# Moving the weight buffers by 32 bytes in SBUF, in a two-block fp32 transformer kernel

## The chip, the cores and the metric

The kernel runs on one core of one Trainium2 chip. The metric is the device time of one execution in microseconds (us). Lower is better.

## What is computed

Two blocks of a transformer-like network on 256 tokens of width 1024, all in fp32. Most of the work is products of the activations with large weight matrices: the input projections, the output projections and five gated feed-forward layers (`f0` to `f4`, hidden width 2816). Cut to what matters:

```python
h = h + (g_a * ya + g_b * yb) @ w_o[l]
hn = rmsnorm(h, norm_ffn_g[l])
gu = hn @ w_ffn_in[l]
g, up = jnp.split(gu, 2, axis=-1)
h = h + (jax.nn.silu(g) * up) @ w_ffn_out[l]
```

Between them stand a banded attention, a gated linear recurrence, a spatial gating unit and a stick-breaking attention. They are small beside the weight products.

## The kernel before

**Splitting.** fp32 accuracy is had from three matmuls per product. Each weight tile `w` is split into `h` (its rounding to float32r, ScalarE, L162) and `l = w - h` (VectorE, L163); activations are split the same way into `xh`, `xl` (or into halves of the four `rr` tables). `mm3` (L212) then issues `h*xh`, `h*xl` and `l*xh` into one PSUM bank. Nearly every matmul of the program is one of these three, issued by `mm` (L210).

**Which operand is which.** In `pe_k`, `pe_a` and `pe_r` (L217 to L238) a 128-column slice of `h` or `l` is the stationary operand, and 256 columns of `xh`, `xl` or `rr` are the moving one. In `pe_nat` and `pe_rn` (L240, L789) it is the other way round: activations are stationary and 512 columns of `h` or `l` move. Half of the kv stage (L916 to L921) moves 256 columns of `h` or `l`. The profile's names put the moving operand first: `wk<-xh,h` moves `xh` over weights `h`.

**Order.** A plan (`make_plan`, L67) fixes the order of all weight tiles. `load` (L139) brings them by DMA on the SP queue, 1 MB (two chunks) at a time, into one of three `raw` tables; `prep` (L149) splits one chunk of 1024 columns per partition into one of eight `h` and eight `l` tables, up to seven chunks ahead of TensorE. One chunk feeds 24 matmuls of `mm3`.

**SBUF layout.** `setup` (L318) allocates the tables of the pool `const` one behind the other, each starting at a multiple of 32 bytes in every partition; the pools `raw` and `hl` (L1243, L1244) follow it. Counted as the remainder of 256 of the start address, before the change:

```
par (896 bytes)                                  128
x0..x3, xh, xl, rr0..rr3, sa                       0
sb, sc, sd, sf, sg, sh, ident, ones              128
rt, r1t, rkv, rckv                               160
half (96 bytes)                                  128
ntri, nones, identb, maskb, lamt                 224
raw, h, l (all buffers)                           64
```

All tables of `x`, `xh`, `xl`, `rr`, `raw`, `h` and `l`, and all their slices that a matmul reads (512 or 1024 bytes apart), are multiples of 256 bytes apart, so one remainder holds for every matmul on them. `ntri` and `nones` are the 128x128 weights of the running sums in `stick` (L1129, L1131); they are used against the `rr` tables.

Of the kernel before, what the change touches and what calls it, by code (L numbers as in the profile page):

```python
# [106 lines left out]
class Builder:  # L107
# [210 lines left out]
    def setup(self):  # L318
        nc, dram = self.nc, self.dram
        self.P = self.sb("par", [128, 224])[:, 0:NPAR]  # L320
        self.X = [self.sb(f"x{p}", [128, 2, 256]) for p in range(4)]
        self.XS = (self.sb("xh", [128, 8, 256], F32R), self.sb("xl", [128, 8, 256], F32R))
        self.RR = [self.sb(f"rr{i}", [128, 8, 256], F32R) for i in range(4)]
        self.SA = self.sb("sa", [128, 2080])[:, 0:8 * 259]
        self.SL = {c: self.sb("s" + c, [128, 2048]) for c in "bcdfgh"}
        self.ident = self.sb("ident", [128, 128])
        self.ones = self.sb("ones", [128, 128])
        self.mhalf = self.sb("mhalf", [128, 2])
        self.Rt = self.sb("rt", [128, 256])
        self.R1 = self.sb("r1t", [128, 256])  # L330
        self.Rkv = self.sb("rkv", [128, 256])
        self.rckv = self.sb("rckv", [128, 16])[:, 0:2]
        self.v2 = self.sb("v2", [128, 2])
        self.rc = self.sb("rc", [128, 2])
        self.tiny = self.sb("tiny", [128, 1])
        self.c8 = self.sb("c8", [128, 8])
        self.nc8 = self.sb("nc8", [128, 8])
        self.half = self.sb("half", [128, 24])
        self.sq = self.view("b", 4)
        nc.scalar.dma_start(self.P, dram["par"])  # L340
        x_load = lambda p: nc.sync.dma_start(self.X[p], dram["x"][:, 2 * p:2 * p + 2, :])
        for f in range(2):
            nc.sync.dma_start(self.X[0][:, f, :], dram["x"][:, f, :])  # L343
        self.warm_up()
        for g in range(2):
            t = self.rawp.tile([128, 2048], F32, tag="raw", name="raw")
            for c in range(2):
                if 2 * g + c:
                    x_load(2 * g + c)
                n = 512 if 2 * g + c == 0 else 1024  # L350
                for o in range(c * 1024, (c + 1) * 1024, n):
                    nc.sync.dma_start(t[:, o:o + n], dram["w"][g, :, o:o + n])  # L352
            self.raw[g] = t
        self.loads = 2
        self.load()
        self.gw = self.SL["h"].rearrange("p (a b) -> p a b", b=128)
        make_identity(nc, self.ident)
        nc.gpsimd.memset(self.ones, 1.0)
        nc.gpsimd.memset(self.mhalf, -0.5)
        nc.gpsimd.memset(self.tiny, 2.0 ** -115)  # L360
# [984 lines left out]
```

## Time and profile before

| | |
|---|---|
| median of 3 runs | 1436.05 us (1435.95 to 1436.43) |
| the profiled execution | 1435.7 us |
| its span, first to last instruction | 1434.0 us |
| mean granted TensorE clock | 0.998 |
| TensorE matmul busy | 1423.5 us, 11548 matmuls |
| VectorE busy | 949.8 us |
| ScalarE busy | 734.9 us |

A matmul's recorded duration is longer than the distance from its start to the next one's, since matmuls are pipelined. What a matmul costs in a dense stream is that distance, here called its step: the length of a piece of the chain divided by its count of matmuls. The recorded duration moves with the step.

### The profile page before, as it was taken

Reading aid. Unit: us, or ns where it says so; the run is one execution under the profiler, and the core shown is the slowest. Engines: PE = TensorE matmul, PEld = TensorE weight load, DVE = VectorE, ACT = ScalarE, POOL = GpSimd, SP = SyncE. Lnnn points to the kernel's source line nnn. Section 1 sums busy time; section 2 is a strip of 40 time slices with the busy share of each in tenths; the row PEclk is TensorE's granted clock in tenths of the full one; section 3 lists DMA queues with packets and bytes.
Section 4 is the critical chain, followed back from the end, with each engine's and each line's share of the span. In section 5 each row is a group of like instructions: output and inputs, shape, how many; then the busy total and the mean of one; then the engine's idle time right before and its main releaser. Section 6 shows DMA issues by size and latency. Waiting matters only on the chain.

```text
span 1434.0 us, 26959 instructions
## 1 busy us (share of the span) xinstructions
PE 1423.5 (99%) x11548; PEld 1384.3 (97%) x11548; DVE 949.8 (66%) x1316; ACT 734.9 (51%) x1094; POOL 24.8 (2%) x57
## 2 busy tenths in 40 slices
PE   9999999999999999999999999999999999999998
PEld 8998989999999999998999999999999998999997
DVE  6976688666557775576776665567655576756663
ACT  5776475544445544455445444446444477544442
POOL 0000000000000000000000000000000000000000
PEclk9999999999999999999999999999999999999999
DMA  8555545454554555546444555544555452445451
GB/s 297 190 204 197 180 171 178 178 204 177 189 193 147 205 182 206 199 165 224 172 163 162 197 186 182 199 178 175 192 199 196 180 176 89 163 155 197 177 190 45
DMA packets 37624, 260.31 MB, mean 182 GB/s; under 512 B 4224, under 2 KB 4608, under 8 KB 7040
## 3 DMA queue, kind: packets, MB, share of 16 engines
q1 hardware_dynamic: 36288, 253.77, 49.5%
q0 software_dynamic: 1072, 4.72, 1.0%
q8 instruction: 90, 1.47, 0.4%
q14 instruction: 30, 0.25, 0.0%
q10 hardware_dynamic: 144, 0.10, 0.0%
HBM read 257.53 MB, written 1.05 MB: 180 GB/s over the span
## 4 chain that ended last, share of the span: by engine, by line
PE 98%; DMA 0%; ACT 0%; DVE 0%; SPq 0%; issue 0%; POOLq 0%; POOL 0%
PE wk L210 62%; PE acc L210 36%; DMA raw<-w 0%; PE acc L521 0%; PE wk L521 0%; ACT sf L959 0%; ACT sd L949 0%; DVE l L163 0%; ACT h L162 0%; SPq L352 0%; SPq L343 0%; DVE sf L950 0%; POOLq L1341 0%; POOL rc L280 0%; ACT sh L1134 0%
## 5 line engine op out<-in xcount | busy, mean ns | idle before, releaser
L163 DVE TENSOR_TENSOR l<-raw,h 128x1024 fp32r<-128x1024 f32 (+1 forms) x479 | 571.1, 1220 | 241.4 <-ACT h L162 241.1
L210 PE MATMUL wk<-xh,h 128*128 128x256 f32 x2272 | 641.1, 282 | 1.8 <-ACT h L162 1.8
L210 PE MATMUL wk<-xh,l 128*128 128x256 f32 x2272 | 638.2, 281 | 0.5 <-DVE l L163 0.5
L210 PE MATMUL wk<-xl,h 128*128 128x256 f32 x2272 | 637.8, 281 | 0.0
L162 ACT ACTIVATE h<-raw 128x1024 fp32r<-128x1024 f32 (+1 forms) x479 | 486.1, 1045 | 61.2 <-PE acc L210 28.8
L210 PEld LDWEIGHTS wk<-xl,h 128*128 128x128 f32 x2272 | 433.2, 191 | 0.5
L210 PEld LDWEIGHTS wk<-xh,h 128*128 128x128 f32 x2272 | 427.4, 188 | 4.5 <-issue 2.0
L210 PEld LDWEIGHTS wk<-xh,l 128*128 128x128 f32 x2272 | 429.8, 189 | 0.9 <-DVE l L163 0.9
L210 PE MATMUL acc<-rr,h 128*128 128x256 f32 x2016 | 359.8, 281 | 0.0
L210 PEld LDWEIGHTS acc<-rr,h 128*128 128x128 f32 x2016 | 309.9, 189 | 1.9 <-issue 1.9
L210 PE MATMUL acc<-rr,l 128*128 128x256 f32 x1008 | 282.8, 281 | 0.0
L210 PEld LDWEIGHTS acc<-rr,l 128*128 128x128 f32 x1008 | 189.9, 188 | 0.0
L738 ACT ACTIVATE sa<-sa 128x256 f32<-128x256 f32 x110 | 45.5, 418 | 271.9 <-DVE sa L306 271.8
L309 ACT ACTIVATE rr<-sa 128x256 fp32r<-128x256 f32 (+1 forms) x122 | 52.7, 439 | 185.3 <-DVE sa L743 128.9
L306 DVE TENSOR_TENSOR sa<-wk,rt 128x512 f32<-128x512 f32 x92 | 62.3, 687 | 79.3 <-PE wk L210 62.6
L310 DVE TENSOR_TENSOR rr<-sa,rr 128x256 fp32r<-128x256 f32 (+1 forms) x122 | 54.1, 451 | 53.4 <-ACT rr L309 53.4
L210 PE MATMUL acc<-h,rr 128*128 128x512 f32 (+1 forms) x208 | 63.1, 374 | 0.0
L210 PEld LDWEIGHTS acc<-h,rr 128*128 128x128 f32 x208 | 38.5, 188 | 7.2
L258 ACT ACTIVATE xh<-x,par 128x256 fp32r<-128x256 f32 x56 | 25.2, 501 | 31.5 <-DVE x L316 16.7
L210 PE MATMUL acc<-l,rr 128*128 128x512 f32 (+1 forms) x104 | 39.1, 376 | 0.0
L743 DVE TENSOR_TENSOR sa<-sa 128x256 f32<-128x256 f32 x88 | 37.1, 429 | 0.0
L210 PE MATMUL wk<-rr,h 128*128 128x256 f32 x192 | 33.0, 277 | 0.0
(253 smaller groups left out, 966.6 us busy)
## 6 DMA issues: line engine op xcount, KB each, us to landing
raw<-w SPq DMA_DIRECT2D x237, 1024.0 KB, 4.9
sd<-bias POOLq DMA_DIRECT2D x8, 384.0 KB, 3.4
raw<-w SPq DMA_DIRECT2D x3, 512.0 KB, 8.4
sh<-gates SPq DMA_DIRECT2D x1, 1024.0 KB, 9.3
out<-sf SPq DMA_DIRECT2D x4, 256.0 KB, 2.2
x<-x SPq DMA_DIRECT2D x3, 256.0 KB, 7.4
raw<-w SPq DMA_DIRECT2D x2, 256.0 KB, 4.5
sa<-ws POOLq DMA_DIRECT2D x1, 512.0 KB, 3.6
```

What stands on the lines that cost most here:

```text
L162: nc.scalar.activation(h[:, s], raw[:, s], AF.Copy)
L163: nc.vector.tensor_tensor(l[:, s], raw[:, s], h[:, s].bitcast(F32), op=ALU.subtract)
L210: self.nc.tensor.matmul(out, lhsT, rhs, start=start, stop=stop, skip_group_check=True)
L258: self.nc.scalar.activation(xs[0][:, k, :], src[p][:, f, :], AF.Copy, scale=self.par(*g(k)))
L306: self.nc.vector.tensor_tensor(dst, bank, self.Rpair(), op=ALU.mult)
L309: self.nc.scalar.activation(zh, src, AF.Copy)
L310: self.nc.vector.tensor_tensor(zl, src, zh.bitcast(F32), op=ALU.subtract)
L738: nc.scalar.activation(t[:, 0, :], t[:, 0, :], AF.Silu)
L743: nc.vector.tensor_tensor(t[:, 1, :], t[:, 0, :], t[:, 1, :], op=ALU.mult)
```

## The change

`setup` gets one more table that nothing reads or writes. It stands behind `half`, so all that is allocated later moves up by 32 bytes: `raw`, `h` and `l` from remainder 64 to 96, and `ntri`, `nones`, `identb`, `maskb`, `lamt` and the small tables behind them likewise by 32 (`ntri` and `nones` from 224 to 0). No instruction is added, removed or moved.

```diff
         self.c8 = self.sb("c8", [128, 8])
         self.nc8 = self.sb("nc8", [128, 8])
         self.half = self.sb("half", [128, 24])
+        self.sb("gap", [128, 8])
         self.sq = self.view("b", 4)
         nc.scalar.dma_start(self.P, dram["par"])
```

## Rows read from the trace of the kernel before

**Rows 1.** The page: busy time of the engines, the granted clock, the chain.
```profile
PE 1423.5 (99%) x11548; PEld 1384.3 (97%) x11548; DVE 949.8 (66%) x1316; ACT 734.9 (51%) x1094; POOL 24.8 (2%) x57
PEclk9999999999999999999999999999999999999999
PE 98%; DMA 0%; ACT 0%; DVE 0%; SPq 0%; issue 0%; POOLq 0%; POOL 0%
```

**Rows 2.** Groups by line and form: operation, out<-in, shapes, count | busy us, mean ns.
```profile
L210 PE MATMUL wk<-xh,h 128*128 128x256 f32 x2272 | 641.1, 282 | 1.8 <-ACT h L162 1.8
L210 PE MATMUL wk<-xh,l 128*128 128x256 f32 x2272 | 638.2, 281 | 0.5 <-DVE l L163 0.5
L210 PE MATMUL wk<-xl,h 128*128 128x256 f32 x2272 | 637.8, 281 | 0.0
L210 PE MATMUL acc<-rr,h 128*128 128x256 f32 x2016 | 359.8, 281 | 0.0
L210 PE MATMUL acc<-rr,l 128*128 128x256 f32 x1008 | 282.8, 281 | 0.0
...
L210 PE MATMUL wk<-rr,h 128*128 128x256 f32 x192 | 33.0, 277 | 0.0
L210 PE MATMUL wk<-rr,l 128*128 128x256 f32 x96 | 26.5, 276 | 0.0
```

**Rows 3.** The chain in order of time, inside f0: start, length, what.
```profile
311.75 11.31 PE wk L210 x96
```

**Rows 4.** The chain, o2 projection and start of f4.
```profile
1230.20 21.76 PE wk L210 x192
```

**Rows 5.** Stretches: window: length, PE busy (matmuls in it), other engines, clock, DMA, GB/s.
```profile
152.00:167.90 15.90, 15.90 (x142) 15.90 (x142) 10.02 (x12) 6.25 (x7) 0.00 (x0) 1.00 0.36 133
230.60:273.90 43.30, 43.30 (x384) 43.30 (x384) 35.07 (x45) 24.97 (x34) 0.00 (x0) 1.00 0.50 185
280.80:461.30 180.50, 180.50 (x1535) 180.50 (x1535) 116.83 (x156) 87.21 (x125) 0.00 (x0) 1.00 0.49 176
683.00:698.50 15.50, 15.50 (x139) 15.50 (x138) 10.76 (x19) 6.13 (x8) 0.72 (x1) 1.00 0.40 145
1229.40:1251.70 22.30, 22.30 (x199) 22.30 (x199) 17.59 (x24) 14.28 (x21) 0.00 (x0) 1.00 0.45 166
```

**Rows 6.** Matmuls on h, 281 to 461 us: count, duration ns min/median/max, first and last start.
```profile
L210 PE MATMUL wk<-xh,h x334: 281/281/281, 280.8 to 460.7; 128*128 128x256 f32 x167
```

**Rows 7.** The same, 231 to 273.9 us.
```profile
L210 PE MATMUL wk<-rr,h x128: 276/276/276, 238.6 to 260.1; 128*128 128x256 f32 x128
```

**Rows 8.** Matmuls on h by window, attention and stick stages: length, PE busy (count), others.
```profile
168.00:230.00 62.00, 46.57 (x257) 38.89 (x256) 19.53 (x17) 16.13 (x16) 1.00 0.53 183
1176.00:1229.00 53.00, 28.09 (x153) 23.07 (x154) 11.35 (x10) 9.52 (x9) 1.00 0.32 109
```

**Rows 9.** Matmuls on h in the kv stage: count, duration ns min/median/max.
```profile
L210 PE MATMUL acc<-h,rr x30: 276/278/283, 1155.0 to 1164.8; 128*128 128x256 f32 x30
```

**Rows 10.** Matmuls on nones: count, duration ns min/median/max.
```profile
L210 PE MATMUL wk<-rr,nones x20: 278/280/282, 1181.3 to 1218.7; 128*128 128x256 f32 x20
```

**Rows 11.** The chain at the end of f4, and pe_nat matmuls on h, 109 to 129 us.
```profile
1416.29 8.27 PE acc L210 x36
...
L210 PE MATMUL wk<-h,xh x29: 392/392/392, 109.3 to 128.5; 128*128 128x512 f32 x29
L210 PE MATMUL wk<-h,xl x29: 388/388/389, 109.8 to 129.0; 128*128 128x512 f32 x29
```

**Rows 12.** The tile raw: its readers and loads, what they waited for, landing.
```profile
L162 ACT ACTIVATE h<-raw x479: 629/1044/1081, 6.0 to 1409.8; 128x1024 fp32r<-128x1024 f32 x159, 128x512 fp32r<-128x512 f32 x1
L163 DVE TENSOR_TENSOR l<-raw,h x479: 691/1224/1230, 6.7 to 1410.9; 128x1024 fp32r<-128x1024 f32 x159, 128x512 fp32r<-128x512 f32 x1
...
  DMA raw<-w: 10.5, 13
...
DMA to landing us min/median/max: 4.3/4.9/9.8
```

## The prediction

> **What bounds the kernel now.** I read the page first: TensorE's matmuls fill 99% of the span, the chain that ended last is 98% TensorE, and the clock was granted in full in every slice [rows 1]. So the time is a count of matmuls times what one costs, and no other engine, queue or transfer sets it. The change adds no instruction; it can act only by changing what an instruction costs because of where its operands lie, or by changing a transfer.
>
> Next, the groups by form: 9,840 matmuls of 256 columns stand in the five large groups and 288 in the two small ones, 10,128 together [rows 2]. Then the chain in order of time, for their step. In f0 it has a piece of 96 matmuls in 11.31 us: a step of 117.8 ns [rows 3]. In the o2 projection and the start of f4 it has 192 of the same shape in 21.76 us: 113.3 ns [rows 4]. The two levels, 4.5 ns apart, are what the reader is to see. They are no mean over disturbed and undisturbed matmuls: from 281 to 461 us every recorded duration on `h` is 281 ns [rows 6], from 231 to 274 us every one is 276 ns [rows 7], a difference that answers to that of the steps. The clock is 1.00 in both kinds of stretch, and the transfers have a like share (0.49 against 0.50 in the two longest shown) [rows 5]. VectorE and ScalarE work at irregular moments, which constant durations do not show; so I read the levels as something between TensorE's own two reads, the moving operand and the next weights, fixed by how the two stand to each other when a stream begins and then kept.
>
> I call them the short step (113.3) and the long step (117.8). How many matmuls are at which? Four stretches of the short step hold 142, 384, 139 and 199 matmuls, 864 [rows 5]. In the attention and stick stages 257 and 153 matmuls read `h` [rows 8], with `l` half as many again, 615; many pieces there are at the short step too, and together with a few shorter stretches elsewhere I take 550 for them, an estimate. That makes about 1,410 matmuls at the short step and, by difference, some 8,700 at the long one.
>
> **The change, part by part.** *The table itself* costs nothing: no instruction reads or writes it.
>
> *The split weights as stationary operand* (10,128 matmuls). Their distance to the moving activations goes from 64 to 96 by the remainder of 256. What does the trace show at other distances? In half of the kv stage `h` moves and the activations at 0 are the weights, a distance of 192: durations 276 to 283 ns, median 278 [rows 9]. Both levels occur there. `nones`, also read against `rr` at 0, has remainder 224, which like the new 96 is an odd multiple of 32: 20 matmuls of 256 columns at 278 to 282, median 280 [rows 10], none at 276. So the long step, within 2 or 3 ns, is found at every distance shown; the short one is found at distances of even multiples of 32 and not at the one odd multiple shown. Twenty matmuls in short runs, with a moving operand in two blocks, are thin evidence, but they are the nearest rows to what the change makes. I take from them that the short step is lost and the long one stays: 1,410 x 4.5 ns = 6.3 us more. The bounds from the same rows: at 278 everywhere the 8,700 gain 3 ns and the 1,410 lose 2, -26 + 3 = -23 us; at 283, the highest of [rows 9], the 8,700 lose 2 ns and the 1,410 lose 7, +17 + 10 = +27 us. Outside these lies the case that all take the short step: 8,700 x 4.5 = -39 us.
>
> *The split weights as moving operand* (the 512-column matmuls of `pe_nat` and `pe_rn`). 36 of them take 8.27 us at the end, 229.7 ns each; their durations in the V stage are 392 and 388 [rows 11], so there are levels here too, 4 ns apart. There are some 550. If all go one such level up or down: 2.2 us either way. I take 0 and keep both ends.
>
> *`ntri` and `nones`* go to remainder 0: some 64 matmuls in the stick stage; at 2 to 6 ns each that is under 0.4 us. I take 0.
>
> *The split on ScalarE and VectorE* reads and writes `raw`, `h` and `l`, which move together. A chunk costs 1.04 us on ScalarE and 1.22 us on VectorE [rows 12] and feeds 24 matmuls, 2.83 us at 117.8 ns. The engines are 51% and 66% busy [rows 1] and work up to seven chunks ahead. That cover hides any change of theirs under about 0.9 us per chunk, the third of VectorE's time that is idle; past it TensorE would wait on `l`.
>
> *The loads into `raw`.* A load lands 4.9 us after its issue [rows 12]; two chunks last TensorE 5.65 us, and three buffers stand behind one another. Everything that waited for loads waited 10.5 us in 13 times [rows 12], ScalarE's own waits, not the chain's. Doubling the landing time would still fit in three buffers. I take 0; at the first loads, which nothing covers, a tenth slower would be half a microsecond.
>
> **The sum**, against the profiled execution of 1435.7 us: +6.3, so 1442.0. The median of the runs stands 0.35 us above that execution, so the forecast is 1442.4 us, 0.4% slower.
>
> A rule speaks against any effect. The granted clock and the issued work are the same on both levels, and yet one shape has two steps [rows 3, 4]. The Trainium skill, SBUF — State Buffer, "Who interferes with whom", states that TensorE and ScalarE never wait on anyone, and TensorE: Matmul & The Clock Gate, Part 2, that loading the next weights takes nothing from the running matmul's reads. By these pages the time would stay at 1436. The trace does not refute them outright, but they have no place for the two levels.
>
> **The rivals.**
>
> *The short step wins (faster).* The mechanism: where a stream begins, the standing of the two reads picks one of two steps that both hold themselves; 32 bytes more may put the long feed-forward stretches, which all begin after the same few small matmuls, on 113.3 ns. For it: they begin alike, so they could flip together; the short step exists and lasts (384 matmuls in one stretch [rows 5]). Against it: nothing at an odd multiple of 32 has it [rows 10]. Price: -39 us, 1397 us. It decides the sign as soon as more matmuls gain the short step than there are to lose it, some 1,410 of 8,700, which is less than one feed-forward layer (1,535 matmuls in the window of [rows 5]). A weaker form, the 278 of [rows 10] everywhere, gives 1413 us.
>
> *Nothing changes (same).* The levels are picked by what ran before a stretch and not by where the tables lie; each stretch keeps its step. For it: the long step is the same, within 2 ns, at three distances [rows 6, 9, 10]. Against: the short one is not. 1436 us.
>
> *A level above 281 (longer still).* With 283 everywhere [rows 9] 1463 us. For it: the rows show it; against: there it comes for single matmuls only, where the moving operand changes from `rr` to `h` and back.
>
> That the change does not move the tables can be left out: `gap` comes ahead of all later tables and pools, and 32 bytes is the unit in which they start.
>
> **How the numbers follow.** A measurement of this kernel can tell about 0.2%, 3 us, from no change. Forecast, the short step lost and the long one kept or raised by up to 1 ns: 0.40, 1438 to 1453 us. A higher level: 0.08. The short step wins in most or all stretches: 0.28; the weaker form: 0.06. Nothing changes: 0.18. So faster 0.34, same 0.18, slower 0.48. The likeliest case's own range is 1438 to 1453. Cases of both signs hold much of the chance, so the range reaches from 1397, the short step everywhere, to 1463, a level of 283 everywhere; what lies outside, other levels than the rows show, I put at under 0.2.
>
> **What would show it.** Right: matmuls on `h` in the stretch from 231 to 274 us and in the o2 projection with durations of 280 to 282 instead of 276, the feed-forward stretches still at 281, the chain still 98% TensorE, the counts the same. Wrong: pieces of 96 matmuls in 10.88 us (113.3 ns) in f0 to f4, or pieces over 11.5 us; or a chain in which waits on `l`, `h` or `raw` appear, which would mean that the cover of VectorE, ScalarE or the loads was thinner than I took it.

## The result, and the profile after

The changed kernel takes 1450.24 us (median of 4 runs, 1449.61 to 1450.78) against 1436.0 us (1435.76 to 1436.43) before: a ratio of 1.0099, interval 1.0081 to 1.0116. The time went up by 14.2 us, where 6.3 us were forecast. The profiled execution took 1450.38 us with a span of 1448.7 us, 14.7 more than before, and that difference is what is accounted for here.

The page after, engines, granted clock and the chain by engine, which answer to [rows 1]:

```profile
PE 1438.5 (99%) x11548; PEld 1397.6 (96%) x11548; DVE 950.6 (66%) x1316; ACT 734.8 (51%) x1094; POOL 25.8 (2%) x57
PEclk9999999999999999999999999999999999999999
...
PE 99%; DMA 0%; ACT 0%; DVE 0%; issue 0%; SPq 0%; POOLq 0%; POOL 0%
```

The counts are the same, the clock is full in every slice, the chain is still TensorE's. VectorE and ScalarE stand within 1 us of what they were. TensorE alone has 15.0 us more of busy time. So no new wait came: matmuls got dearer.

The tile `raw`, which answers to [rows 12], shows that the other engines' cover held: what ScalarE and VectorE need for a chunk and what a load takes to land have not moved.

```profile
L162 ACT ACTIVATE h<-raw x479: 629/1045/1081, 6.4 to 1424.3; 128x1024 fp32r<-128x1024 f32 x159, 128x512 fp32r<-128x512 f32 x1
L163 DVE TENSOR_TENSOR l<-raw,h x479: 692/1224/1227, 7.1 to 1425.3; 128x1024 fp32r<-128x1024 f32 x159, 128x512 fp32r<-128x512 f32 x1
...
  DMA raw<-w: 11.6, 13
...
DMA to landing us min/median/max: 4.7/4.9/9.7
```

The chain in order of time (start, length, what) shows the steps. First f0, then f1, f2, the o2 projection and start of f4, and the end of f4:

```profile
316.10 11.27 PE wk L210 x96
...
487.23 11.52 PE wk L210 x96
...
823.28 11.39 PE wk L210 x96
...
1243.18 22.53 PE wk L210 x192
...
1430.79 8.43 PE acc L210 x36
```

Divide length by count. Before, f0 had 117.8 ns [rows 3]; now f0 has 117.4, f1 120.0, f2 118.6. The piece of 192, at 113.3 before [rows 4], is at 117.3. The 512-column matmuls at the end went from 229.7 ns [rows 11] to 234.2. One long step has become at least three, and the piece of 192 has lost the short one.

The recorded durations of matmuls on `h` (count, ns min/median/max, first and last start) say more about the kind of step. From 234 to 278 us (answers [rows 7]), from 285 to 466 (answers [rows 6]), in f1 and in f2:

```profile
L210 PE MATMUL wk<-rr,h x128: 277/280/283, 241.8 to 264.1; 128*128 128x256 f32 x128
...
L210 PE MATMUL wk<-xh,h x337: 277/280/366, 285.3 to 466.0; 128*128 128x256 f32 x169
...
L210 PE MATMUL wk<-xh,h x295: 282/283/283, 473.0 to 630.7; 128*128 128x256 f32 x148
...
L210 PE MATMUL wk<-xh,h x332: 276/282/283, 809.2 to 989.7; 128*128 128x256 f32 x166
```

Before, the two stretches of [rows 6, 7] had one duration each, 281 and 276. Now f1 has one, 282 to 283, at a step of 120.0; the others go through a pattern of 276 to 283 that repeats, and 117.3 or 118.7 is its mean. The windows of f0 and f1 now, and of f1 before in the last line (length, busy time and count of each engine, clock, share of the DMA engines, GB/s):

```profile
285.30:466.00 180.70, 180.70 (x1543) 180.70 (x1542) 117.51 (x157) 87.21 (x125) 0.00 (x0) 1.00 0.49 176
473.00:642.00 169.00, 169.00 (x1411) 169.00 (x1410) 109.09 (x137) 78.22 (x110) 2.56 (x2) 1.00 0.55 196
...
469.00:635.40 166.40, 166.40 (x1415) 166.40 (x1414) 109.48 (x138) 78.69 (x111) 2.55 (x2) 1.00 0.55 199
```

The transfers take a larger share in f1 than in f0 (0.55 against 0.49), but they did so before too (0.55 in the last line, 0.49 in [rows 5]), when both layers had 117.8 ns. So they do not explain 117.4 against 120.0.

**Where the 14.7 us come from.** Each matmul of the one trace was set beside the same matmul of the other, and the distances to the next start compared. For 256 columns, distances of 100 to 140 ns in both traces are counted, and up to 114.5 ns before is short:

| matmuls | count | mean step before | after | us |
|---|---|---|---|---|
| 256 columns, at the short step before | 1,418 | 113.3 | 117.9 | +6.4 |
| 256 columns, at the long step before | 8,877 | 117.8 | 118.5 | +6.5 |
| 512 columns | 548 | 229.7 | 233.3 | +2.0 |
| the rest | | | | -0.1 to -0.2 |

The first line is the forecast's one term; the second and third were put at nothing.

### The profile page after: what moved, and what is told of

It reads as the page before. It is cut to its first block, busy times and chain, and to the rows that moved or that the text cites. A ratio compares the mean times of both kernels' runs of the same rounds, so it can differ in the third digit from the quotient of the medians.

```text
span 1448.7 us, 26959 instructions
## 1 busy us (share of the span) xinstructions
PE 1438.5 (99%) x11548; PEld 1397.6 (96%) x11548; DVE 950.6 (66%) x1316; ACT 734.8 (51%) x1094; POOL 25.8 (2%) x57
## 4 chain that ended last, share of the span: by engine, by line
PE 99%; DMA 0%; ACT 0%; DVE 0%; issue 0%; SPq 0%; POOLq 0%; POOL 0%
PE wk L210 62%; PE acc L210 36%; DMA raw<-w 0%; PE acc L522 0%; PE wk L522 0%; ACT sf L960 0%; ACT sd L950 0%; SPq L344 0%; DVE sf L951 0%; DVE l L163 0%; ACT h L162 0%; POOLq L1342 0%; POOL rc L280 0%; ACT sh L1135 0%; DVE v L955 0%
```

## The experiments

All kernels start from the kernel before, but for the last two, which start from the changed one. Unused tables move things: a pool `gapa` ahead of the pool `raw` moves `raw`, `h` and `l`; a pool `gapb` between `raw` and `hl` moves `h` and `l` alone; `ntri` and `nones` stay where they were. "Distance" is the remainder of 256 of the start of the weights less that of the activations: 64 before, 96 after.

### Which tables matter

**Only `h` and `l` to 96**, `raw` left at 64:

```diff
             tc.tile_pool(name="raw", bufs=NRAW) as rawp, \
+            tc.tile_pool(name="gapb", bufs=1) as gb, \
...
+        gb.tile([128, 8], F32, tag="gapb", name="gapb")
```

> Only h and l move by 32 bytes (remainder 96); raw stays at 64, ntri and nones at 224. If TensorE's two reads carry the effect (theory): 1448 to 1451 us, no step of 113.3 ns left in the stretch that runs from 231 to 274 us before. If ScalarE's and VectorE's work on raw or the loads into it carry it: within 2 us of 1436.

Measured: 1449.98 us (1449.57 to 1450.51), ratio 1.0099 (1.0082 to 1.0116), the whole effect.

**Only `raw` to 96**, `h` and `l` at 64: `gapa` of 32 bytes, `gapb` of 224.

```diff
+        ga.tile([128, 8], F32, tag="gapa", name="gapa")
...
+        gb.tile([128, 56], F32, tag="gapb", name="gapb")
```

> Only raw moves by 32 bytes (remainder 96); h and l stay at 64, now at other absolute addresses. Theory of TensorE's two reads: within 2 us of 1436, matmul durations on h of 281 and 276 as before. If the loads or the split carry the effect: 1448 to 1451 us.

Measured: 1436.21 us, ratio 1.0004 (0.9995 to 1.0013), no change in the time. The chains of these two kernels at the start of f1, first with `h` and `l` moved, then with `raw` moved:

```profile
487.76 11.52 PE wk L210 x96
```

```profile
483.44 11.31 PE wk L210 x96
```

The first has the step of the changed kernel, 120.0 ns, the second that of the kernel before, 117.8. So the loads into `raw` and the reads of `raw` by ScalarE and VectorE have no part in it, nor have `ntri` and `nones`, which the first kernel leaves alone. Writes of `h` and `l` moved too, but the next kernel bears on them. One stretch did change with `raw` alone: the piece of 192 in the o2 projection and the start of f4 has 117.8 ns, where it had 113.3 before [rows 4].

```profile
1230.62 22.62 PE wk L210 x192
```

It is worth 0.9 us. The distance is the same, 64, so a stretch can change its step without a change of distance.

**Everything up by 32 bytes**, activations and weights alike, so the distance stays 64:

```diff
+        self.sb("gap0", [128, 8])
         self.P = self.sb("par", [128, 224])[:, 0:NPAR]
```

> Everything moves by 32 bytes, activations to remainder 32 and weights to 96: their distance is 64 again. If the distance of the two operands of a matmul decides: within 3 us of 1436, with steps of 113.3 and 117.8 ns. If the weights' own remainder of 96 decides (a start that is an odd multiple of 32): 1448 to 1451 us and no 113.3 ns.

Measured: 1435.83 us, ratio 1.0000 (0.9991 to 1.0010). `h` and `l` lie at 96 as in the changed kernel, their writers and loads see the same places, and nothing is lost. What counts is where the weights lie against the activations, and TensorE's matmuls are what reads both. ScalarE and VectorE write both, and their writes could meet TensorE's reads; the trace of the changed kernel speaks against it. In f1, 107 matmul steps begin and end while neither of the two engines works, with a mean of 120.0 ns; in 209 both work throughout, and the mean is 120.0 too. In f0 the means are 117.3 and 117.4.

**256 bytes more** under `raw`, `h` and `l`:

```diff
+        ga.tile([128, 64], F32, tag="gapa", name="gapa")
```

> raw, h and l move by 256 bytes: the remainder of 256 stays 64, that of 512 changes. If the period is 256: within 2 us of 1436. If any other place of the buffers gives another pick of levels: more than 4 us away from 1436, to either side.

Measured: 1435.84 us, ratio 1.0000 (0.9991 to 1.0010). At this distance 256 bytes more change nothing, so the remainder of 256 is what is counted here.

### The other distances

`gapa` of 64, 96, 128, 160, 192 and 224 bytes gives distances 128, 160, 192, 224, 0 and 32. The edit for 160:

```diff
+        ga.tile([128, 24], F32, tag="gapa", name="gapa")
```

> raw, h and l move by 64 bytes: 128 past the activations, an even multiple of 32. Theory (even multiples of 32 keep the short step of 113.3 ns, odd ones lose it): matmuls of 113.3 ns present, 1397 to 1442 us. Rival (64 is special, any other distance is worse): no 113.3 ns, 1445 us or more.

> Weights 160 past the activations, an odd multiple of 32. Theory of even and odd: no matmul step of 113.3 ns, long steps of 117 to 120, 1442 to 1458 us. Rival (64 alone is special): the same. Rival (no order in it, each place a new pick): 113.3 ns occurs.

> Weights 192 past the activations, that is 64 ahead of them. The theory of even and odd has fallen. Theory (64 to either side is special): matmuls of 113.3 ns present, within 1400 to 1445 us. Rival (only 64 behind is special): no 113.3 ns, 1447 to 1467 us.

> Weights 224 past the activations, 32 ahead of them. Theory (the short step needs a distance of 64): no 113.3 ns, steps of 117 to 122, 1445 to 1467 us. Rival (the nones matmuls at 224 in the kernel before, 278 to 282 ns, say what all would do): long steps of 115 to 119, 1413 to 1445 us.

> Weights at the same remainder as the activations, distance 0. Theory of even and odd: 113.3 ns present, 1397 to 1442 us. Rival (two reads at the same remainder meet in the same place): the longest of all, over 1458 us.

> Weights 32 past the activations, an odd multiple of 32. Theory of even and odd: no 113.3 ns, 1442 to 1458 us. Rival (no order in it): 113.3 ns occurs.

Measured, with 64 and 96 for comparison; the mean steps are from the starts of all matmuls of that width in the trace, "short" counts 256-column steps up to 114.5 ns out of some 10,300:

| distance | us | ratio (interval) | mean step, 256 columns | 512 columns | short |
|---|---|---|---|---|---|
| 0 | 1462.40 | 1.0183 (1.0168 to 1.0198) | 119.95 | 227.4 | 34 |
| 32 | 1448.96 | 1.0089 (1.0074 to 1.0104) | 118.3 | 233.3 | 23 |
| 64 (before) | 1436.0 | 1 | 117.2 | 229.7 | 1,419 |
| 96 (after) | 1450.24 | 1.0099 (1.0081 to 1.0116) | 118.4 | 233.3 | 177 |
| 128 | 1454.50 | 1.0127 (1.0110 to 1.0144) | 118.9 | 232.7 | 52 |
| 160 | 1466.17 | 1.0209 (1.0194 to 1.0224) | 119.94 | 234.0 | 22 |
| 192 | 1443.01 | 1.0062 (1.0045 to 1.0079) | 117.7 | 233.3 | 202 |
| 224 | 1436.72 | 1.0013 (1.0004 to 1.0023) | 117.1 | 233.3 | 1,267 |

The chain shows what stands behind the means. Distance 0, f0:

```profile
302.22 11.52 PE wk L210 x96
```

Distance 224, f0 and f1:

```profile
316.10 11.31 PE wk L210 x96
...
504.10 11.20 PE wk L210 x96
```

At 0 nearly every step in the program is 120 ns. At 160 every long stretch has 120.0 as its mean, of single steps from 115 to 125 ns, and at 32 every one has 118.3. At the other distances the step differs from stretch to stretch. At 224 f0 has 117.8 and f1 116.7, and the short steps counted there are single ones: in f1 the starts go 113, 116, 118, 120 in turn. No stretch holds 113.3 at 224. Long stretches at 113.3 ns stand at 64 alone; at 192 there is one, of 94 matmuls, and everywhere else in its long stretches 192 has 117.8, as 64 has. The recorded durations differ all the same. Here are f0's chain and its matmuls on `h`, first at 192, then at 160:

```profile
314.57 11.31 PE wk L210 x96
...
L210 PE MATMUL wk<-xh,h x321: 279/279/279, 284.7 to 460.0; 128*128 128x256 f32 x161
```

```profile
303.11 11.52 PE wk L210 x96
...
L210 PE MATMUL wk<-xh,h x325: 279/286/286, 290.0 to 470.0; 128*128 128x256 f32 x163
```

A step of 117.8 ns goes with 279 ns at 192 and with 281 at 64 [rows 3, 6]. So "the recorded duration moves with the step" holds within one distance only; a duration at one distance does not tell the step at another.

Against what was expected: the reading by even and odd multiples of 32 does not survive this, since 0 and 128 are even, have no short stretch and took 1462 and 1454 us where 1397 to 1442 were expected. Of the odd ones 32 came inside its 1442 to 1458, 160 above it. At 0 the time is over 1458 us, but not the longest of all. At 192 the time lies in the 1400 to 1445 expected if 64 to either side is special, but few steps are short. At 224 the reading from `nones` met the time, and the one by which the short step needs 64 expected at least 1445. With one start for each distance the table does not say that such a stretch can't occur there, only that it did not.

### Where a stream begins

At one distance the step can be 113.3 or 117.8 from stretch to stretch. Does the start in time pick it? Eight extra matmuls of 64 columns, one in each call of `stats_b`, into columns of the statistics bank that nobody reads, in the layout of before:

```diff
+        self.mm(self.st[:, 0, 128:128 + 64], self.identb, self.identb[:, 0:64], False, True)
```

> The layout of before; one matmul of 64 columns that nobody reads is put ahead of each of the broadcast matmuls that come before the long feed-forward stretches. Theory (where the stream starts in time picks the step, the distance only says which steps there are): in some of the stretches of f0 to f4 the step is another than before, 113.3 instead of 117.8, 5 to 30 us less. Rival (the distance alone decides): every stretch keeps its step, within 2 us of 1436.

> As the run with 64 columns, but with 68: streams start 4 columns later. Theory of the start: the stretches at 113.3 are others than with 64 columns or before, times between 1400 and 1440 us. Rival: within 2 us of 1436, as with 64.

Measured: 1406.75 us with 64 columns (1406.18 to 1407.28), ratio 0.9808 (0.9794 to 0.9823), and 1407.54 us with 68, ratio 0.9819 (0.9800 to 0.9837). Work was added, and 29 us went. With 68 columns all five feed-forward layers changed as with 64, where others were expected; only short stretches in the first 50 us differ, some 200 matmuls. So four columns more do not pick another step for the layers. The page and the chain of the kernel with 64, from f0, f1 and f2:

```profile
PE 1393.4 (99%) x11556; PEld 1353.7 (96%) x11556; DVE 949.2 (68%) x1316; ACT 735.0 (52%) x1094; POOL 24.7 (2%) x57
...
310.57 10.88 PE wk L210 x96
...
475.91 10.88 PE wk L210 x96
...
833.56 10.88 PE wk L210 x96
```

Pieces of 96 in 10.88 us are 113.3 ns. All five feed-forward layers hold it: 8,174 steps are short against 1,419, and (8,174 - 1,419) x 4.5 ns = 30.4 us, against 29.0 us of span, 1434.0 to 1405.0. No table moved. That it is the start in time that picks, and not something else that the small matmul changes ahead of the stream, is not shown. The gating unit kept the long step, as durations of 281 on `h` show there (276 in the layers):

```profile
L210 PE MATMUL acc<-rr,h x256: 281/281/364, 719.2 to 766.1; 128*128 128x256 f32 x128
...
L210 PE MATMUL acc<-rr,h x340: 276/276/276, 289.8 to 439.9; 128*128 128x256 f32 x170
```

**The same in the gating unit too**: beside the eight, one extra 64-column matmul ahead of the four of each `mix` group.

```diff
+            self.mm(bank[:, 0, 0:64], self.identb, self.identb[:, 0:64], True, True)
```

> The layout of before with the extra matmul ahead of the broadcasts and one more ahead of the four of each group in the gating unit, which are followed by 117.8 ns both before and with the 64 columns. Theory of the start: some of these stretches, some 660 matmuls, change to 113.3 ns: 1403 to 1407 us. Rival (they stay): 1407 us.

Measured: 1420.15 us (1419.93 to 1420.22), ratio 0.9890 (0.9876 to 0.9905): better than before, 13.4 us worse than with the eight alone. The gating unit did not change its step, and f2 and f3, which come later, went back to the long one:

```profile
836.02 11.31 PE wk L210 x96
```

Their 2,960 or so matmuls x 4.5 ns = 13.3 us, which is the loss. Right ahead of f2 and f3 stands the same extra matmul as in the kernel with eight. The last of the new ones starts at 729 us and f2 at about 788, so what runs earlier decides how a later stream starts, over more than 50 us. Neither reading had foreseen the time (1403 to 1407, or 1407).

**The start at distance 96**: does the changed kernel have a short step that its starts just miss? The table of the change, and the eight extra matmuls with 64 and with 72 columns:

```diff
+        self.sb("gap", [128, 8])
...
+        self.mm(self.st[:, 0, 128:128 + 64], self.identb, self.identb[:, 0:64], False, True)
```

> The layout of the change (distance 96) with the extra matmul of 64 columns ahead of the broadcasts. Theory (the distance says which steps exist, the start picks among them; 96 has no short step): no 113.3 ns in any long stretch, only a new pick among 117.3, 118.7 and 120, 1440 to 1462 us. Rival (96 has the short step too, the change only picked another start): 113.3 ns in f0 to f4, 1406 to 1430 us.

> As the last, with 72 columns, so another start. Theory: again no 113.3 ns, 1440 to 1462 us, the three long steps spread otherwise over the stretches. Rival: 113.3 ns in some stretches, below 1436 us.

Measured: 1447.16 us with 64 columns, ratio 1.0081 (1.0064 to 1.0098), and 1446.88 with 72, ratio 1.0076 (1.0061 to 1.0091). The chain with 64 columns, f0 and f1:

```profile
316.12 11.39 PE wk L210 x96
...
488.70 11.27 PE wk L210 x96
```

f0 went from 117.4 to 118.6 and f1 from 120.0 to 117.4: the start picks anew, but among the steps that the changed kernel already showed. 24 and 28 steps are short. So three starts at distance 96 gave no stretch at 113.3, where the same extra work at 64 gave it in every feed-forward layer.

## Why the prediction was right or wrong

**What bounds the kernel, and which resource could act: right as far as the runs reach.** "Something between TensorE's own two reads, the moving operand and the next weights" is where the first four kernels point. Moving `raw` alone or everything together leaves the time as it was, moving the weights against the activations does it all. What goes on inside TensorE's reads was not seen; no run tells why 64 has a step of 113.3 and 0 has 120.0.

**The short step is lost: right in size.** 1,410 matmuls x 4.5 ns = 6.3 us were forecast, 1,418 and 6.4 us were found. The count by windows and the step from the chain were good enough.

**"The long one stays": this step failed.** 8,700 matmuls were to stay at 117.8 ns, taken from durations that lay "within 2 or 3 ns" at every distance shown. At distance 96 the long steps are 117.3, 118.7 and 120.0. Layer by layer, f0 gained 0.7 us while f1 lost 3.1, f2 1.4 and f3 1.3, and in all the long ones cost +6.5 us, as much as the whole forecast. On 8,900 matmuls 0.7 ns on average is 6 us, so a duration good to 2 ns could not carry a term of zero; the text had that bound, 283 for 281, and kept it for the range alone. Its likeliest case allowed "up to 1 ns", which covers 1450, but the sum took nothing of it. One of its own signs of being wrong came: a piece of 96 over 11.5 us, 11.52 in f1.

**The evidence for it, `nones` [rows 10], was of another distance.** 224 was read as standing for 96 because both are odd multiples of 32. The sweep has 224 itself: 117.8 and 116.7, with durations of 277 to 281 in the long streams, near the 278 to 282 of `nones`. The row told of its own distance well and of 96 nothing, and the median of 280 at 224 goes with 117.8 in f0 there, as 281 does at 64 and 279 at 192. That odd ones have no stretch at 113.3 agrees with all four odd distances; that even ones do is not borne out by 0 and 128. The short step was lost as forecast, by a rule that does not hold.

**The 512-column matmuls** were taken at 0 with bounds of 2.2 us either way: +2.0 us came, near the upper one. `ntri` and `nones`, the split, the loads: taken at 0 and not to be seen, as the kernel with only `h` and `l` moved has the same time as the changed one.

**The rivals.** The short step did not win here, but its mechanism, that a stream takes one of two steps as it begins and then holds it, is shown by the eight extra matmuls; what was missing is that the distance first says which steps there are to pick from, as far as the starts tried at 96 tell. "Nothing changes" fell. By the Trainium skill, SBUF — State Buffer, "Who interferes with whom", TensorE never waits on anyone. On the other engines the trace agrees, with 120.0 ns in f1 whether ScalarE and VectorE work or not. But that the time would stay does not follow: it is 1435.83 us at one distance and 1450.24 at another for the same instructions. "A level above 281" came in part: f1 stands at 283, with 1463 us as its price if all had gone there. At distance 0, where the layers did, the time was 1462; 160 has the same mean step of 120.0 with unequal durations and took 1466.

## What to carry to other kernels

Where a dense stream of matmuls sets the time, divide pieces of the chain by their counts and compare the steps of one shape: two levels at a full clock are time to be had. Scan the place of the weights against the activations in 32-byte units with an unused pool, and scan how the streams start with a tiny extra matmul ahead of them; here the eight matmuls gave 1406.75 us, 29 us under the kernel before and 43 under the changed one. Scan again after any edit upstream, since one in the gating unit undid the gain in two layers behind it.

## What the runs showed that was not expected

Distances 0 to 224 in units of 32 bytes span 1436 to 1466 us, 2.1%, with instructions unchanged. Adding eight matmuls takes 2% off. At distances 0 and 160 the 256-column matmuls are at their longest, 119.95 and 119.94 ns, but the 512-column ones, in which the weights move, are at their shortest at 0, 227.4, and at their longest at 160, 234.0. Four of 56 executions of the kernel before took 1432.3 to 1432.8 us and the others 1435.1 to 1437.2. Some 700 matmuls at the short step instead of the long one would make the 3 us; none of the four was profiled, so that is not shown. What makes a repeating pattern of steps at one distance and a constant one at another stays open, and so does whether a start exists at 32, 128, 160 or 224 that holds 113.3 ns: it was not tried.
